# One of four input slots moved 128 B off a multiple of 512 B, in a batched matmul that is bound by its transfers

## The chip, the cores and the metric

The kernel runs on one core of one Trainium2 chip. The metric is the device time of one execution in microseconds (us), the median of several runs. All quoted comparisons are between runs marked fast, made on the same chip in the same call, except where it is said that a run stands alone (its state is then unknown).

## The reference

```python
# a: (16, 512, 512) float32 as (batch, k, m);  b: (16, 512, 512) float32 as (batch, k, n)
def reference(a, b):
    return np.matmul(a.transpose(0, 2, 1), b).astype(np.float32)
```

The inputs are 33.55 MB and the output is 16.78 MB: 50.33 MB have to cross between memory and the core's SBUF.

## The kernel before

The 16 products are made in 8 pairs. A load brings one operand (a or b) of one pair, 2 MiB, into one of four input slots: 16 KiB on each of 128 partitions. VectorE casts it to bfloat16, TensorE multiplies, ScalarE takes the sums out of PSUM into an output tile, and when the loads are over the stores follow. All DMAs are issued by the sync engine (SP) and share one queue.

```python
NX = 4
done = pool.tile([1, 96], f32, name="done")          # 384 B; 24 columns are used
x_ts = [pool.tile([P, R, M], f32, name=f"x{j}") for j in range(NX)]      # P 128, R 8, M 512
abf_ts = [...]; bbf_ts = [...]; o_ts = [...]         # (cut)
...
for n in range(2, 2 * pairs):                        # load n: a if n is even, b if it is odd
    if n >= NX:
        nc.sync.wait_ge(s_in, n - NX + 1)            # the slot has been cast
    nc.sync.dma_start(x_ts[n % NX][:], in_v[n % 2][n // 2]).then_inc(s_x[n % NX], 16)
...
nc.vector.wait_ge(s_x[n % NX], 16 * (n // NX + 1))   # for each pair (cut)
nc.vector.tensor_copy(out=(bbf_ts if n % 2 else abf_ts)[v][:],
                      in_=x_ts[n % NX][:, v * RV:(v + 1) * RV, :]).then_inc(s_cast, 1)
```

The slots begin at multiples of 512 B within a partition. Four small constants take 128 B ahead of the flag tile `done`, and its 384 B make up the rest.

Of the kernel before, what the change touches and what calls it, by code (L numbers as in the profile page):

```python
# [8 lines left out]
def kernel(  # L9
# [7 lines left out]
    P = 128  # L17
    batch, K, M = a.shape
    _, _, N = b.shape
    f32 = mybir.dt.float32  # L20
# [7 lines left out]
    R = K // Q  # L28
# [14 lines left out]
    NX = 4  # L43
# [4 lines left out]
    pool = ctx.enter_context(tc.tile_pool(name="sb", bufs=1))  # L48
# [2 lines left out]

    done = pool.tile([1, 96], f32, name="done")
    dve_done, act_done = done[:, 0:2 * pairs], done[:, 2 * pairs:3 * pairs]
    x_ts = [pool.tile([P, R, M], f32, name=f"x{j}") for j in range(NX)]
    abf_ts = [pool.tile([P, RV, M], bf, name=f"abf{v}") for v in range(V)]
    bbf_ts = [pool.tile([P, RV, N], bf, name=f"bbf{v}") for v in range(V)]
    o_ts = [pool.tile([P, G, T, N], f32, name=f"o{j}") for j in range(NO)]
# [157 lines left out]
```

## Time and profile before

| | before |
|---|---|
| median of the runs beside the first measurement | 123.78 us |
| span in the profile | 122.0 us |
| time of all DMA packets, share of 16 engines' span | 97.8% |
| packets of 16,384 B in the 14 full loads | 1,792 (8 a load and engine), median 611 ns |
| last product out of PSUM, last store landed | 94.0 us, 121.1 us |

The page tells which resource is full: a share near 100% for the DMA engines and about half for TensorE. The trace also keeps a record of each DMA packet (start, duration, size) and the time of each of the sixteen increments by which a DMA's semaphore tells that it has landed (the last of them is the landing). Among the packets are 448 of 4 B, sixteen for each of the 28 DMAs; I read them as the sending of these increments, one by each engine when it is through with its part.

### The profile page before, as it was taken

Reading aid. Unit: us, or ns where it says so; the run is one execution under the profiler, and the core shown is the slowest. Engines: PE = TensorE matmul, PEld = TensorE weight load, DVE = VectorE, ACT = ScalarE, POOL = GpSimd, SP = SyncE. Lnnn points to the kernel's source line nnn. Section 1 sums busy time; section 2 is a strip of 40 time slices with the busy share of each in tenths; the row PEclk is TensorE's granted clock in tenths of the full one; section 3 lists DMA queues with packets and bytes.
Section 4 is the critical chain, followed back from the end, with each engine's and each line's share of the span. In section 5 each row is a group of like instructions: output and inputs, shape, how many; then the busy total and the mean of one; then the engine's idle time right before and its main releaser. Section 6 shows DMA issues by size and latency. Waiting matters only on the chain. (4 is left out here: it accounts for less than half of the span.)

```text
span 122.0 us, 1208 instructions
## 1 busy us (share of the span) xinstructions
PE 63.6 (52%) x480; PEld 35.2 (29%) x480; DVE 37.9 (31%) x48; ACT 32.1 (26%) x41; POOL 0.2 (0%) x4
## 2 busy tenths in 40 slices
PE   0006928379969649979919928946991000000000
PEld 0002304135546325636606605612550000000000
DVE  0042070680494092474355437419000000000000
ACT  4000332400570830191570390191048000000000
POOL 0000000000000000000000000000000000000000
PEclk9999999958999995999999999995899855555555
DMA  4999999999999999999999999999999999999994
GB/s 97 363 424 430 448 430 440 430 430 435 435 430 435 430 430 430 430 430 430 430 430 430 435 430 430 430 365 430 430 422 430 427 430 427 427 430 427 430 430 180
DMA packets 5056, 50.33 MB, mean 412 GB/s; under 512 B 448, under 2 KB 448, under 8 KB 960
## 3 DMA queue, kind: packets, MB, share of 16 engines
q1 hardware_dynamic: 5056, 50.33, 97.8%
HBM read 33.55 MB, written 16.78 MB: 412 GB/s over the span
## 5 line engine op out<-in xcount | busy, mean ns | idle before, releaser
L147 PE MATMUL ps<-bbf,abf 64*128 64x512 bf16 x448 | 54.3, 401 | 15.3 <-PEq L142 15.3
L147 PEld LDWEIGHTS ps<-bbf,abf 64*128 64x128 bf16 x448 | 31.4, 114 | 38.2 <-issue 23.5
L172 ACT COPY o<-ps 128x1024 f32<-128x1024 f32 x28 | 26.3, 1027 | 43.9 <-PE ps L147 43.9
L109 DVE CAST abf<-x 128x2048 bf16<-128x2048 f32 x14 | 17.1, 1224 | 17.4 <-PE ps L147 13.4
L109 DVE CAST bbf<-x 128x2048 bf16<-128x2048 f32 x14 | 17.1, 1224 | 16.5 <-DMA x<-in_b_dram 16.5
L127 PE MATMUL ps<-bbf,abf 128*128 128x512 bf16 x32 | 9.3, 456 | 13.1 <-PEq L125 13.1
L127 PEld LDWEIGHTS ps<-bbf,abf 128*128 128x128 bf16 x32 | 3.8, 124 | 18.1 <-issue 16.2
L166 ACT COPY o<-ps 128x1024 f32<-128x1024 f32 x4 | 4.1, 1014 | 17.2 <-PE ps L127 17.2
L93 DVE CAST abf<-x 128x2048 bf16<-128x2048 f32 x2 | 2.5, 1228 | 11.9 <-PE ps L127 6.0
L93 DVE CAST bbf<-x 128x2048 bf16<-128x2048 f32 x2 | 2.4, 1224 | 1.7 <-DMA x<-in_b_dram 1.7
L177 ACT ACTIVATE done<-done 1x1 uint32<-1x1 uint32 x8 | 1.6, 197 | 0.0
L166 ACT ACT_TABLE_LOAD x1 | 1.3, 1283 | 0.9 <-SPq L71 0.9
L115 DVE MEMSET done<- 1x1 f32 x14 | 0.8, 59 | 0.0
L97 DVE MEMSET done<- 1x1 f32 x2 | 0.1, 59 | 0.0
L199 POOL MEMSET const-uint8-127<- 128x1 uint8 x1 | 0.1, 102 | 0.0
L199 POOL MEMSET const-bfloat16-1.0<- 128x1 bf16 x1 | 0.1, 101 | 0.0
L199 POOL MEMSET const-float32-0.0<- 128x1 f32 x1 | 0.1, 98 | 0.2 <-issue 0.2
L199 POOL MEMSET const-float32-1.0<- 128x1 f32 x1 | 0.1, 98 | 0.0
## 6 DMA issues: line engine op xcount, KB each, us to landing
out_dram<-o SPq DMA_DIRECT2D x8, 2048.0 KB, 25.0
x<-in_a_dram SPq DMA_DIRECT2D x7, 2048.0 KB, 12.1
x<-in_b_dram SPq DMA_DIRECT2D x7, 2048.0 KB, 15.9
x<-in_a_dram SPq DMA_DIRECT2D x1, 1024.0 KB, 8.4
x<-in_b_dram SPq DMA_DIRECT2D x1, 1024.0 KB, 10.4
x<-in_a_dram SPq DMA_DIRECT2D x1, 768.0 KB, 4.5
x<-in_b_dram SPq DMA_DIRECT2D x1, 768.0 KB, 6.5
x<-in_a_dram SPq DMA_DIRECT2D x1, 256.0 KB, 2.7
```

Of the source, the lines that this page charges most:

```text
L93: nc.vector.tensor_copy(out=bf_ts[0][:], in_=x_ts[j][:, u * RV:(u + 1) * RV, :]).then_inc(s_cast, 1)
L97: nc.vector.memset(dve_done[:, j:j + 1], 0.0).then_inc(s_in, 1)
L109: nc.vector.tensor_copy(out=(bbf_ts if n % 2 else abf_ts)[v][:], in_=x_ts[n % NX][:, v * RV:(v + 1) * RV, :],).then_inc(s_cast, 1)
L115: nc.vector.memset(dve_done[:, n:n + 1], 0.0).then_inc(s_in, 1)
L127: mm = nc.tensor.matmul(ps_ts[0][h][:, t % 2, :], a_m[:, r, t], bbf_ts[0][:, r, :], start=(r == 0), stop=(r == RV - 1),)
L147: mm = nc.tensor.matmul(ps_ts[g][h][:, t % 2, :], a_m[:, t], bbf_ts[v][rows, r, :], start=(v == 0 and r == 0), stop=(v == V - 1 and r == R ...
L166: nc.scalar.copy(out=o_ts[0][:, g, 2 * h:2 * h + 2, :], in_=ps_ts[0][h][:]).then_inc(s_ev[h], 1)
L172: ev = nc.scalar.copy(out=o_ts[i % NO][:, g, 2 * h:2 * h + 2, :], in_=ps_ts[g][h][:])
L177: nc.scalar.memzero(act_done[:, i:i + 1]).then_inc(s_out, 1)
L199: nc = _bacc.Bacc("TRN2", target_bir_lowering=False, num_devices=1)
```

## The change

The intent is to see what the start address of an input slot within a partition is worth, with everything else left in place. The second gap restores the alignment of what lies behind.

```diff
-    x_ts = [pool.tile([P, R, M], f32, name=f"x{j}") for j in range(NX)]
+
+    x_ts = [pool.tile([P, R, M], f32, name=f"x{j}") for j in range(NX - 1)]
+    pool.tile([1, 32], f32, name="gap0")
+    x_ts.append(pool.tile([P, R, M], f32, name=f"x{NX - 1}"))
+    pool.tile([1, 96], f32, name="gap1")
```

## The prediction

> **What bounds the kernel now.** I read the page first, then the view of waits of the queue that issues the DMAs, then the chain of work that ended last, then the windows view by stage, the source view of the load line, and at the end the trace's record of every DMA packet.
>
> ```profile
> PE 63.6 (52%) x480; PEld 35.2 (29%) x480; DVE 37.9 (31%) x48; ACT 32.1 (26%) x41; POOL 0.2 (0%) x4
> DMA  4999999999999999999999999999999999999994
> GB/s 97 363 424 430 448 430 440 430 430 435 435 430 435 430 430 430 430 430 430 430 430 430 435 430 430 430 365 430 430 422 430 427 430 427 427 430 427 430 430 180
> DMA packets 5056, 50.33 MB, mean 412 GB/s; under 512 B 448, under 2 KB 448, under 8 KB 960
> q1 hardware_dynamic: 5056, 50.33, 97.8%
> ```
>
> No compute engine is busy for much over half of the 122.0 us, while the DMA engines are busy in every slice but the first and the last, at 97.8% over the span. They move 430 GB/s nearly throughout. So this is a DMA-bound kernel from the third slice to the end, and any time added to the packets is added to the end, if nothing else leaves a gap in the queue.
>
> ```profile
> 94.02 0.06 ACT done L177
> ```
>
> The chain view's last entry is ScalarE's last flag, at 94.0 us, 28 us before the end. What follows is only the wait for the stores:
>
> ```profile
> SPq L80 <- DVE done L115: 44.0, 10, 8.3
> SPq L210 <- DMA out_dram<-o: 26.4, 1, 26.4
> ```
>
> Loads do wait for slots (44.0 us in ten waits), but the windows view shows that this waiting is ahead of need: the DMA share stays at 1 in each stretch.
>
> ```profile
> 40.00:50.00 10.00, 7.33 (x54) 4.01 (x51) 3.71 (x6) 3.82 (x5) 0.00 (x0) 0.83 1.03 442
> 78.00:82.00 4.00, 2.65 (x26) 1.39 (x21) 0.54 (x2) 3.07 (x4) 0.00 (x0) 1.00 0.94 375
> 94.00:110.00 16.00, 0.00 (x0) 0.00 (x0) 0.00 (x0) 0.07 (x2) 0.00 (x0) 0.58 1.01 428
> ```
>
> The last three columns are the clock of TensorE, the DMA share and GB/s. Only 78 to 82 us is under full rate: there the last load ends and the first store begins. The source view of the load line confirms the lead:
>
> ```profile
> DMA to landing us min/median/max: 10.9/14.6/19.0
> ```
>
> A 2 MiB load by itself takes 4.9 us, so each is issued two to four loads ahead of its landing.
>
> The packet records give the unit of cost. A full load is 128 packets of 16,384 B, 8 on each of 16 engines, and a packet takes 611 ns (median of 1,792). Packets of 8,192, 6,144 and 2,048 B take 309, 234 and 84 ns. That is a line: 8 to 9 ns fixed, and 1.177 ns for each 32 B ((611 - 309) / 256). At 16,384 B there are 512 such steps. There is no sign of a cost per 256 or 512 B beyond the steps themselves. All input slots now begin at multiples of 512 B, as the change says, so the trace has no misaligned load to look at.
>
> **What the Trainium skill says.** First, "DMA: Bandwidth & Descriptors", section "Where 436 GB/s comes from": 16 ports x 32 B x 850 MHz is 435.2 GB/s, so 1.176 ns for each 32 B. The trace agrees: 1.177 ns a step, and 430 GB/s in most slices. The kernel before sits on that ceiling. Second, the same page, section "How a descriptor splits into AXI transactions": a descriptor is cut into transactions of 256 B that begin at multiples of 256 B. One that begins off such a multiple has a first piece from the boundary below and a leftover at the end, and the bytes ahead of the start still cost beats. Its examples are about fetching; the write side isn't told apart, and no run so far shows either. Third, "SBUF — State Buffer", section "Operand start alignment": DMAs put the intended bytes at any element-aligned address, and "these runs timed nothing". It is about legality, so it says only that the result stays right. Fourth, "DMA: Bandwidth & Descriptors", section "Specifications": transfers under 512 B are done as read-modify-write. No data packet here is under 2 KB, so the trace shows nothing of that.
>
> **The change part by part.** It adds no instruction, removes none and moves no wait. It adds 128 B before the fourth input slot and 384 B behind it, 512 B together, so all tiles behind keep their place relative to 512 B. The memory is there, since no tile shrinks.
>
> What changes is the destination of one slot. Slots are used in turn, four of them, and there are 16 operand loads (two of them split in three parts). The fourth slot therefore takes loads 3, 7, 11 and 15: four loads of b, not the last alone. That is 4 x 2 MiB = 8.4 MB of the 50.3 MB, or 4 x 8 = 32 packets of 16,384 B on each engine: 32 x 611 ns = 19.6 us of DMA time. The HBM side of these loads keeps its alignment, and so do all stores.
>
> By the second place of the skill a 16,384 B packet that begins 128 B past a multiple of 256 B touches 65 pieces of 256 B and not 64. At worst each packet pays one piece more: 611 / 64 = 9.5 ns. 32 packets x 9.5 ns = 0.31 us. If only the half piece of bytes at an edge is paid, it is 0.15 us, and if the writes carry no unused bytes (128 B is four whole steps of 32 B), it is zero.
>
> Beside the DMA: VectorE reads this slot in 8 casts (v = 0 and 1 of four pairs) of 1,224 ns. The operand stays aligned to its elements and contiguous, so I give this zero; if a cast did grow, VectorE is 31% busy and issues loads about two loads ahead of need. Nothing of the DMA cost is hidden, though. The queue is one and first-in first-out in practice, always filled, so slower packets push every later load and every store. The last store is issued at 94.2 us and its data does not begin to move until about 116.6 us (the six stores before it must go first), so the compute tail has some 22 us to spare and hides nothing and adds nothing. The sum is 123.78 + 0.31 = 124.09, and I say 124.1 us.
>
> **The rivals.**
>
> First: every piece pays, not the packet's edge alone. The data arrive from HBM in aligned pieces of 256 B and each must be written across a boundary, as 128 + 128 B. If each cut costs one dead step, a packet gains 64 x 1.177 = 75 ns, 32 packets 2.4 us, and the time is 126.2 us. With three dead steps for each it is 7.2 us and 131.0 us. If the write rate halves, it is 19.6 us and 143.3 us. Against this: the packets of four sizes show a pure cost by 32 B steps, so pieces of 256 B go without a gap now, and 128 B is a whole number of steps. For it: nothing in the trace shows a misaligned write, the DMA has no slack to hide one, and somebody rounded the little flag tile up to 96 columns where it uses 24, which is what brings the slots to multiples of 512 B. That looks like a choice made for a reason.
>
> Second: the partial 512 B at each end of a row is done as read-modify-write. Two small ends a packet, if not overlapped, might cost as much as two of the smallest data packets seen, 2 x 84 ns (an estimate). Then 32 x 168 ns = 5.4 us and 129.2 us. Against: packets follow each other and such an end should overlap with the next packet.
>
> Third: nothing at all is seen, or a little gain. Only the ends could gain: the fixed 9 ns of 32 packets is 0.29 us, and the dip to 365 GB/s in one slice of 3.05 us at the last load is worth 65 / 430 x 3.05 = 0.46 us, if the new offset happened to remove it. So even the best case is about 123.0 us, 0.6%, and faster by over 2% is as good as excluded.
>
> Fourth: only the last load matters, because it alone gates the last products. Then a slower load would be hidden in the 22 us to spare. I don't believe it: its DMA time is in the queue before the stores.
>
> **Range and chances.** The main step gives 123.8 to 124.1, and run-to-run spread is 0.1 us. The first and second rival pull up, to 126 to 131 and in a tail further. I take 64% for a cost of under 2.4 us (edges, nothing, or a fraction of a dead step for each piece), 35% for over 2%, and 1% for a gain over 2%. The range is 123.5 to 130.0; what lies above it is the case of a write rate that falls by a third or more for this slot.
>
> **What would show it.** Right: the 16,384 B packets of loads 3, 7, 11 and 15 at 611 to 621 ns, the spacing of landings of these loads 4.9 us, slices all near 430 GB/s, the same packet count, casts at 1,224 ns. Wrong, first rival: these four loads alone lengthen by the same amount each, with four stretches of lower GB/s at a DMA share that stays at 1, and the span grows by their sum. Second rival: the same four, by a fixed amount a packet, which a half-size packet would show too. Wrong in another way: other loads or the stores change, or the queue runs dry (a DMA share under 1 in mid-span), which would mean that the lead of two loads is not enough; or more packets of another size, if the descriptors are cut differently at the new address.

## The result, and the profile after

The changed kernel took 123.63 us (median of four runs, 123.48 to 123.75) against 123.78 us (123.69 to 123.82). The ratio is 0.9988 with a 95% interval of 0.9971 to 1.0005: the same. A ratio is the mean time of one kernel's fast runs over that of the other's in the same rounds, so it isn't quite the ratio of the medians.

The page of the changed kernel, the lines on busy time, DMA by slice, packets and the queue:

```profile
PE 64.9 (53%) x480; PEld 35.3 (29%) x480; DVE 38.0 (31%) x48; ACT 32.1 (26%) x41; POOL 0.2 (0%) x4
DMA  4999999999999999999999999999999999999994
GB/s 96 364 435 427 462 430 430 430 430 435 430 430 430 430 430 430 430 430 430 430 430 430 430 430 435 424 373 427 430 422 430 430 430 427 427 430 427 427 430 180
DMA packets 5057, 50.33 MB, mean 413 GB/s; under 512 B 449, under 2 KB 449, under 8 KB 961
q1 hardware_dynamic: 5056, 50.33, 97.8%
```

The data packets are as many as before and the DMA share is the same; the one packet more belongs to another queue (instructions). One caution on the GB/s row: 430 in a slice of 3.05 us is 80 packets of 16,384 B, so the row moves by whole packets, in steps of about 5 GB/s, and can't show a difference of half a per cent.

The waits of the issuing queue:

```profile
SPq L84 <- DVE done L119: 43.1, 10, 8.8
SPq L214 <- DMA out_dram<-o: 27.1, 1, 27.1
```

The last entry of the chain that ended last:

```profile
92.59 0.06 ACT done L181
```

These answer to 44.0 us, 26.4 us and 94.0 us before. The loads still wait for slots far ahead of need. The compute tail ended 1.4 us earlier, which bought nothing, because the stores behind it were still in the queue: the last one landed at 121.0 us, against 121.1 us before.

The windows view of the changed kernel; the last columns are the TensorE clock, the DMA share and GB/s:

```profile
78.00:82.00 4.00, 4.00 (x40) 2.58 (x36) 1.37 (x2) 1.43 (x2) 0.00 (x0) 1.00 0.96 379
94.00:110.00 16.00, 0.00 (x0) 0.00 (x0) 0.00 (x0) 0.00 (x0) 0.00 (x0) 0.52 1.01 429
```

The dip where the last load meets the first store is there as before (379 GB/s against 375), so the offset did not remove it. The packet records say the rest. In loads 3, 7 and 11, which go to the moved slot, every one of the 384 packets takes 611 ns, as do all packets of the other full loads but the last. The sharpest look is at the time between two landings in the moved slot, which a cast of b waits for. The timeline of VectorE, casts of loads 7 and 11, first before, then after:

```profile
42.90 1.23 DVE L109 CAST bbf<-x 128x2048 bf16<-128x2048 f32 x1 [3.33 <-DMA x<-in_b_dram]
...
62.35 1.23 DVE L109 CAST bbf<-x 128x2048 bf16<-128x2048 f32 x1 [3.34 <-DMA x<-in_b_dram]
```

```profile
42.84 1.23 DVE L113 CAST bbf<-x 128x2048 bf16<-128x2048 f32 x1 [2.81 <-DMA x<-in_b_dram]
...
62.29 1.23 DVE L113 CAST bbf<-x 128x2048 bf16<-128x2048 f32 x1 [1.77 <-DMA x<-in_b_dram]
```

The first column is the start in us. 62.35 - 42.90 and 62.29 - 42.84 are both 19.45 us for a round of four loads. The edges that the prediction charged would have shown as 8 x 9.5 ns = 0.08 us in this difference, and the step here is 0.01 us.

### The profile page after: what moved, and what is told of

Its sections match the earlier page's. It is cut to its first block, busy times and chain, and to the rows that moved or that the text cites. A ratio compares the mean times of both kernels' runs of the same rounds, so it can differ in the third digit from the quotient of the medians.

```text
span 122.0 us, 1208 instructions
## 1 busy us (share of the span) xinstructions
PE 64.9 (53%) x480; PEld 35.3 (29%) x480; DVE 38.0 (31%) x48; ACT 32.1 (26%) x41; POOL 0.2 (0%) x4
## 5 line engine op out<-in xcount | busy, mean ns | idle before, releaser
L151 PE MATMUL ps<-bbf,abf 64*128 64x512 bf16 x448 | 53.0, 394 | 12.6 <-PEq L146 12.6
L113 DVE CAST abf<-x 128x2048 bf16<-128x2048 f32 x14 | 17.1, 1224 | 19.5 <-PE ps L151 13.9
L113 DVE CAST bbf<-x 128x2048 bf16<-128x2048 f32 x14 | 17.1, 1224 | 13.4 <-DMA x<-in_b_dram 13.4
L131 PE MATMUL ps<-bbf,abf 128*128 128x512 bf16 x32 | 11.9, 553 | 13.0 <-PEq L129 13.0
L97 DVE CAST bbf<-x 128x2048 bf16<-128x2048 f32 x2 | 2.4, 1224 | 1.8 <-DMA x<-in_b_dram 1.8
```

Source lines behind the costliest of these rows:

```text
L97: nc.vector.tensor_copy(out=bf_ts[0][:], in_=x_ts[j][:, u * RV:(u + 1) * RV, :]).then_inc(s_cast, 1)
L131: mm = nc.tensor.matmul(ps_ts[0][h][:, t % 2, :], a_m[:, r, t], bbf_ts[0][:, r, :], start=(r == 0), stop=(r == RV - 1),)
L151: mm = nc.tensor.matmul(ps_ts[g][h][:, t % 2, :], a_m[:, t], bbf_ts[v][rows, r, :], start=(v == 0 and r == 0), stop=(v == V - 1 and r == R ...
```

## The experiments

The question was whether an offset costs nothing at all or costs something that this kernel hides. Theory 1 is that only whole steps of 32 B count. The rivals are an edge paid by each packet, a cost by every piece, and a gain. Out of the first batch came theory C: the writing side does pay, but makes up for it in the loads to the slots that are not off.

**Once more, with five rounds.** No edit: the changed kernel.

> The changed kernel once more, beside the kernel before on the same chip, to see whether the 0.15 us by which it was quicker is real. If a 128 B offset costs and gains nothing (theory 1): ratio 1.000 within 0.001, every 16,384 B packet of loads 3, 7, 11 and 15 at 611 ns. If there is a small gain by the offset (theory 2): again about 0.9988, with an interval below 1. If an edge is paid (theory 3, as predicted): up to 1.0025.

Measured: 123.91 us against 123.88 us; the ratio is 0.997 (0.9929 to 1.0011). The runs of the kernel before spread over 123.59 to 125.32 us, so the interval is wide. The packets of loads 3, 7 and 11 took 611 ns, all of them. The 0.15 us of the first measurement is not shown to be a gain: the medians are level here, and both intervals hold 1.

**All four slots 128 B off.** Each slot gets 128 floats more, and a view of it begins 32 floats in:

```diff
-    x_ts = [pool.tile([P, R, M], f32, name=f"x{j}") for j in range(NX)]
+    OFF = 32
+    raw_ts = [pool.tile([P, R * M + 128], f32, name=f"x{j}") for j in range(NX)]
+    x_ts = [t[:, OFF:OFF + R * M].rearrange("p (r m) -> p r m", r=R) for t in raw_ts]
```

> All four input slots begin 128 B past a multiple of 512 B: four times the dose. Theory 1 (the write side counts whole steps of 32 B and an offset of four steps costs nothing): 16,384 B packets at 611 ns in all 14 full loads, the 2,048, 6,144 and 8,192 B packets at 84, 234 and 309 ns, time within 0.1% of before. Theory 3 (an edge of 9.5 ns a packet, hidden by chance in one slot): 14 x 8 packets x 9.5 ns = 1.1 us more for the full loads, 124.9 us. Theory 2 (a gain by the offset): about 4 x 0.15 = 0.6 us less.

Measured: 124.20 us against 123.88 us; ratio 0.9992 (0.995 to 1.0033). But the packets moved: their mean rises from 612.8 and 612.1 ns in the first two full loads to 614.6 ns in loads 6 to 14. So theory 1 falls, and the edge of theory 3 exists at 3.6 ns, not at 9.5 ns (the spacing of the slots changed as well; it is tested below).

**All four slots 4 B off.** The same edit with `OFF = 1`.

> All four input slots begin 4 B past a multiple of 512 B, so no write of a load begins at a whole step of 32 B. Theory 1a (a packet is streamed and only its edges are partial): one step more a packet, 1.2 ns, 14 x 8 x 1.2 = 0.13 us, which is in the noise; packets at 611 to 613 ns. Theory 1b (each 256 B piece from the source is written apart, and touches 9 steps of 32 B for 8): 64 x 1.177 = 75 ns a packet, 8.4 us in all, about 132 us, packets at 686 ns. Casts may be slower at 4 B past, which the slack of the load queue would hide.

Measured: 124.45 us against 123.88 us; ratio 1.0015 (0.9973 to 1.0056). Packets take 616.6 ns in the mean, 5.6 ns more, in nearly all loads from the first. Theory 1b (75 ns) falls, and theory 1a, which gave 611 to 613 ns, is too small. So 4 B, which breaks the 32 B step, costs 2.0 ns more than 128 B, and the casts still take 1,224 to 1,225 ns.

**Reading 128 B further in memory**, slots at multiples of 512 B, wrong result:

```diff
-            nc.sync.dma_start(x_ts[n % NX][:], in_v[n % 2][n // 2]).then_inc(s_x[n % NX], 16)
+            src = in_v[n % 2][n // 2]
+            if n < 2 * pairs - 2:
+                flat = (a, b)[n % 2].rearrange("b k m -> (b k m)")
+                at = (n // 2) * G * K * M + 32
+                src = flat[at:at + G * K * M].rearrange("(p r m) -> p r m", p=P, r=R)
+            nc.sync.dma_start(x_ts[n % NX][:], src).then_inc(s_x[n % NX], 16)
```

> Wrong result on purpose: 12 of the 14 full loads read 128 B further in memory, the slots stay at multiples of 512 B. The fetch side, of which the skill's examples speak. If the bytes ahead of the start cost beats: 512 + 4 steps, 616 ns a packet, 12 x 8 x 4.7 = 0.45 us more. If a whole piece is paid: 620 ns and 0.9 us. If only whole steps count: 611 ns and no change.

Measured: 123.85 us against 123.88 us; ratio 0.9968 (0.9915 to 1.0021). The median packet takes 611 ns in each load. Some packets are longer (up to 751 ns), but loads 4, 5, 8 and 9, all read off, are at 611 ns to the last packet. No cost of the bytes ahead of the start is to be seen on the fetching side. Whether it is absent or hidden behind another limit, no run here tells.

**A control for the spacing.** The wide spacing with `OFF = 0`.

> A control for the two kernels with all four slots off: the same spacing of the slots as there (16,896 B and not 16,384 B), but all slots at multiples of 512 B. If the 3.5 ns more a packet of the kernel with all slots at 128 B comes from the offset (theory A): 611 ns for all full loads here, and the time as before. If it comes from the spacing of the slots (theory B): about 614.5 ns here too.

Measured: 123.64 us against 123.89 us; ratio 0.9981 (0.9929 to 1.0033). All full loads but the last are at 611 ns. The spacing costs nothing.

**All four slots off in the tight spacing:**

```diff
-    done = pool.tile([1, 96], f32, name="done")
+    done = pool.tile([1, 128], f32, name="done")
...
     x_ts = [pool.tile([P, R, M], f32, name=f"x{j}") for j in range(NX)]
+    pool.tile([1, 96], f32, name="gap1")
```

> All four slots 128 B past a multiple of 512 B, in the spacing of the kernel before (16,384 B). Theory A (the offset): mean 614 to 615 ns a packet in the full loads after the first few, 0.3 to 0.4 us more in all. Theory B (the spacing): 611 ns and no change.

Measured: 123.99 us against 123.89 us; ratio 0.9999 (0.9946 to 1.0052). Packets take 614.6 ns in loads 6 to 14, as with the wide spacing, after two loads still at 611 ns. So it is the offset (theory A), and it takes some loads until it shows. The timelines of VectorE, loads 7 and 11 once more, first of the control, then of the tight kernel with all slots at 128 B, then of the one with all at 4 B:

```profile
42.51 1.23 DVE L111 CAST bbf<-x 128x2048 bf16<-128x2048 f32 x1 [3.33 <-DMA x<-in_b_dram]
...
61.96 1.23 DVE L111 CAST bbf<-x 128x2048 bf16<-128x2048 f32 x1 [3.34 <-DMA x<-in_b_dram]
```

```profile
43.09 1.23 DVE L110 CAST bbf<-x 128x2048 bf16<-128x2048 f32 x1 [3.37 <-DMA x<-in_b_dram]
...
62.68 1.23 DVE L110 CAST bbf<-x 128x2048 bf16<-128x2048 f32 x1 [3.37 <-DMA x<-in_b_dram]
```

```profile
43.34 1.23 DVE L111 CAST bbf<-x 128x2048 bf16<-128x2048 f32 x1 [3.39 <-DMA x<-in_b_dram]
...
62.99 1.23 DVE L111 CAST bbf<-x 128x2048 bf16<-128x2048 f32 x1 [3.39 <-DMA x<-in_b_dram]
```

A round of four loads takes 19.45, 19.59 and 19.65 us. The 0.14 and 0.20 us over 32 packets are 4.4 and 6.2 ns a packet, with a rounding of 0.3 ns. These are times of the engine that is last. In the mean of the sixteen engines, from the 4 B packets of load 7 to those of load 11, a round takes 19,449 ns before, and 19,577 and 19,651 ns here: 4.0 and 6.3 ns a packet. That is a little more than the packets' own durations show (3.6 and 5.6 ns). The records of neighbouring packets overlap by some 3 ns, so the count from start to start is the surer one.

**Two slots of four 128 B off** (the third and the fourth; `gap0` one slot earlier, and the gap behind as in the change).

> The third and the fourth slot 128 B off, so two loads off are followed by two that are not. If the cost of a load that is off is paid at once, packets of these loads take about 614.5 ns and the others 611 ns. If the write side lags behind and makes up for it in the loads that are not off (theory C, the reason for which one slot of four showed nothing), all packets take 611 ns still, or only the second load off grows a little. If it can't make up, the cost per load off appears from mid-run on, and in aligned loads too.

Measured: 123.79 us in one run, where the kernel before had a median of 123.89 us. All packets from load 4 to load 14 take 611 ns. But the lag grows from round to round. The lag of a load is the time from an engine's 4 B packet to its increment, in the mean of the sixteen engines. For loads 3, 7 and 11 it is 388, 410 and 428 ns. Over the nine pairs of loads to the same slot between load 2 and load 14, it grows by 17 to 22 ns a round, 19 ns in the mean. In the kernel before the same three lags are level at 341 to 343 ns, in the changed one at 359 to 362 ns. So the cost of loads that are off is there, but nothing waits for it yet.

(The expectation of the three-slot run below says 30 ns. That came from the end of the last of a load's 128 packets in order of start. The sixteen engines stand 0.4 to 1.2 us apart in these runs, in all but one kernel more than the 0.6 us of a packet, so packets of the next load get into that count. The lags in this text are by the 4 B packets, whose loads are 4.9 us apart and can't be mixed up.)

**One slot 4 B off** (wide spacing, the fourth slot alone with an offset of one float).

> Only the fourth slot is off, by 4 B and not by 128 B, spacing 16,896 B. With all four slots off by 4 B a packet took 616.6 ns in the mean, 5.5 ns more. Theory C (made up for in the three loads that follow): 611 ns in all loads. If a load off by 4 B is paid at once: 616.6 ns in loads 3, 7, 11 and 15 and 611 ns in the others, 32 x 5.5 = 0.18 us in all.

Measured: 123.88 us in one run. Loads 3, 7 and 11 are at 611 ns to the last packet and their lag is level. The lag shows both halves of theory C. In the load that is off it is 29 ns above that of the kernel before in the same slot, and in the three loads that follow 18, 13 and 1 ns above: it is paid back before the next load that is off. The changed kernel, 128 B off, shows the same with 18, 8, 1 and 1 ns. So one load off in four costs nothing in time, by 4 B as by 128 B.

**Three slots of four 128 B off** (`gap0` behind the first slot).

> Three of the four slots 128 B off. A forecast from theory C with the numbers so far. With all four off, a packet takes 614.6 ns, 3.6 ns more than the 611 ns at which packets are read. With two of four off the lag from the last packet to the landing grew by some 30 ns for each round of four loads, 16 x (3.6 - r), which gives r = 1.7 ns a packet that a slot not off makes up. Three of four: the lag grows by 8 x (3 x 3.6 - 1.7) = 73 ns a round at first, and once there is no room for more, packets take 611 + (3 x 3.6 - 1.7) / 4 = 613.3 ns in the mean. If the cost is paid by each load for itself: 614.6 ns in loads of slots 1, 2 and 3 and 611 ns in those of slot 0. If nothing short of all four costs: 611 ns.

Measured: 124.64 us in one run, against a median of 124.36 us. The forecast held in its sum, not in its order of lag first and packets later. From loads 2 to 5 to loads 6 to 9 the lag grew by 32 ns (73 forecast), and the packets of loads 6 to 9 took 613.2, 612.4, 611.2 and 611.4 ns already: together 32 + 8 x (2.2 + 1.4 + 0.2 + 0.4) = 66 ns (a few of these packets were held up, to 682 ns at most, as single packets of aligned kernels are too). From loads 6 to 9 to loads 10 to 13 the lag grew by 27 ns, while the packets of loads 10 to 13 grew to 613.1, 613.6, 611.4 and 611.5 ns, 612.4 ns in the mean (613.3 forecast). Both together are 27 + 8 x (2.1 + 2.6 + 0.4 + 0.5) = 72 ns a round. So the forecast sum holds, and the room for the lag was filling up. Neither "each load pays for itself" nor "only all four cost" fits. Load 12 goes to the slot that is not off, and load 13 directly behind it is off and still short of paying. The timelines of loads 7 and 11, with two slots off and with three:

```profile
42.95 1.23 DVE L112 CAST bbf<-x 128x2048 bf16<-128x2048 f32 x1 [3.37 <-DMA x<-in_b_dram]
...
62.42 1.23 DVE L112 CAST bbf<-x 128x2048 bf16<-128x2048 f32 x1 [3.35 <-DMA x<-in_b_dram]
```

```profile
43.09 1.23 DVE L112 CAST bbf<-x 128x2048 bf16<-128x2048 f32 x1 [2.70 <-DMA x<-in_b_dram]
...
62.63 1.23 DVE L112 CAST bbf<-x 128x2048 bf16<-128x2048 f32 x1 [1.67 <-DMA x<-in_b_dram]
```

A round takes 19.47 and 19.54 us. With 19.45 us for none and for one, and 19.59 us for four, this is how the time of a round answers to the number of slots that are off.

| kernel | slots off, by | mean packet, loads 10 to 13 | lag of loads 3, 7, 11, mean of the engines |
|---|---|---|---|
| before | none | 611.0 ns | 342, 341, 343 ns |
| control, wide | none | 611.0 ns | 342, 340, 343 ns |
| changed | one, 128 B | 611.0 ns | 362, 359, 360 ns |
| one slot, wide | one, 4 B | 611.0 ns | 370, 371, 371 ns |
| third and fourth | two, 128 B | 611.0 ns | 388, 410, 428 ns |
| second to fourth | three, 128 B | 612.4 ns | 408, 441, 467 ns |
| all, tight | four, 128 B | 614.6 ns | 470, 477, 478 ns |
| all, wide | four, 128 B | 614.6 ns | 452, 482, 482 ns |
| all, wide | four, 4 B | 616.6 ns | 463, 464, 463 ns |

The lag of an aligned load depends on its slot and hardly on the kernel: in the four kernels with all input slots aligned it is 339 to 348 ns for loads 3 and 4 and those to the same slots, and 319 to 325 ns for the other two slots (load 15 left out). So the level can be read too. With one or two slots off the lag stays at or under 428 ns, and packets keep 611 ns from load 4 on, but for two stray ones. With three slots off it goes from 416 to 469 ns in loads 6 to 14, and packets grow in part of the loads. With all four 128 B off it comes to rest at 475 to 483 ns from load 5 on, while every load pays.

**Short rows, slots at multiples of 512 B**, as a magnifier for a cost by edges. The loads of the fourth slot come in runs of 512 B; the cast and its wait follow suit (cut):

```diff
+            if n % NX == NX - 1:
+                dst = x_ts[n % NX][:].rearrange("p r m -> p (r m)").rearrange("p (h r m) -> p h r m", h=4, r=R)
+                src = in_v[n % 2][n // 2].rearrange("p r (h m) -> p h r m", h=4)
+                for h in range(4):
+                    nc.sync.dma_start(dst[:, h], src[:, h]).then_inc(s_x[n % NX], 16)
+                continue
```

> A magnifier, slots at multiples of 512 B: the four loads of the fourth slot are brought in runs of 512 B (32 for each partition) by four issues each, and the cast puts them in order again, so the result stays right. By the line of packet times, 8.5 ns + 16 x 1.177 ns = 27.3 ns a packet, 256 a load and engine: 7.0 us a load for 4.9, and 4 x 2.1 = 8.4 us more in all, 132 us. It is the base for the next one.

Measured: 127.95 and 128.54 us in two fast runs, 134.39 and 134.74 us in two slow. In the profiled fast run a load in short rows takes 6.05 us from the landing before it to its own, where 7.0 us was expected, so the base came out lower than the sum of its packet times.

**Short rows, the fourth slot 128 B off**: the same edit on the changed kernel.

> The same runs of 512 B, with the fourth slot 128 B off as in the changed kernel. If an offset of 128 B costs 3.6 ns for each packet on the write side (an edge): 256 x 4 x 3.6 = 3.7 us more than with the slot at a multiple of 512 B, less what the other loads make up. If a whole further piece of 256 B is paid for each packet: 9.5 ns and 9.7 us more. If the cost is by bytes and not by edges (3.6 ns for 16,384 B): nothing to be seen. If partial 512 B are read and written back, far more, 20 us and up.

Measured: 132.42 to 132.80 us in four fast runs; ratio to the kernel before 1.0657 (1.0613 to 1.07). Against the mean of the two fast runs at multiples of 512 B, 128.25 us, the mean of 132.66 us is 4.4 us more. That is 4.4 us / 1,024 packets = 4.3 ns a packet. This fits a cost by edges (3.7 us expected), and neither a cost by bytes (nothing) nor a read-modify-write (20 us and up). It isn't settled: the aligned kernel's own slow runs, at a granted clock of 0.83 and 0.84 like the fast ones (0.83 and 0.85), lie above these times, I don't know what makes them slow, and the profile of this kernel fell in a slow run, so I read no line of it.

**Output tiles 128 B off**, input slots aligned (a gap of 32 floats ahead of the output tiles).

> The output tiles 128 B off, the input slots at multiples of 512 B: stores read the slot off a multiple of 256 B. If fetching pays the bytes ahead of the start, as the skill's examples have it: 8,192 B packets of the stores at 309 + 4 x 1.177 = 314 ns, 128 x 4.7 = 0.6 us more in all. If the fetch side pays nothing, as loads from 128 B further in memory did not: 309 ns. ScalarE's evictions stay at 1,027 ns.

Measured: 123.89 us in one run, against a median of 124.36 us. The 8,192 B packets of the stores stay at 309 ns and the evictions at 1,026 ns. Reading a slot off a multiple of 256 B costs nothing that shows.

## Why the prediction was right or wrong

**The bound: right.** The kernel stayed bound by its transfers, the queue never ran dry and the compute tail had time to spare, which is seen in its ending 1.4 us earlier for nothing.

**The range and the chances: right.** 123.63 us lies in the range, and "within 2%" had the largest chance. It lies near the low end, though, under the 123.8 to 124.1 of the main step, whose cost was not there. The runs after it gave no reason for the 35% on slower: with rows of 16 KiB even four slots off stay within 0.6% by their intervals.

**The sum: one term too large.** The step "At worst each packet pays one piece more: 611 / 64 = 9.5 ns" gave 0.31 us. For one slot the term measured zero in the packets and in the time. An edge does exist, at 3.6 ns a packet when all four slots are off (4.0 ns from start to start). The lower ends that the same step named, 0.15 us and zero, were nearer. Two readings of the prediction are slightly off, and nothing hangs on them: (611 - 309) / 256 is 1.180 ns and not 1.177, and when the last store is issued five of the seven stores ahead of it have still to land, not six, and its own first packets start at 115.4 us and not 116.6.

**The step that failed** is "Nothing of the DMA cost is hidden". It holds for the queue, which has no gap, but not within a transfer. A packet whose write costs some ns more does not hold up the next packet at once: what shows is a later landing. In the changed kernel the lag is 18 ns higher after the load that is off, 8 ns after the next one and 1 ns after that, and the round takes the same 19.45 us. That is why one slot shows nothing in the packets or in the time. The two-slot run gives the net of a round. Its lag grows by 19 ns for 16 packets off and 16 not, so 16 x (3.6 - r) = 19 and the rate r at which aligned loads make up is about 2.4 ns a packet (an estimate from these two numbers). Three slots off should then cost 8 x (3 x 3.6 - 2.4) = 67 ns a round, and 66 and 72 ns were measured. Within a round the rates are rough: one load off should add 8 x 3.6 = 29 ns, and 18 were seen. That the lag is a lag of writes behind reads is my reading of it. The records show when a packet ends and when its DMA lands, not which side of the transfer they time. What sets the room for this lag, some 140 to 160 ns above the lag of aligned loads in the same slot, stays open as well. With all slots 4 B off it is a little smaller (460 to 465 ns) though a packet costs more.

**The first rival** (each piece of 256 B pays, 75 ns a packet) is refuted even at 4 B off, where a packet takes 5.6 ns more. **The second** (read-modify-write of both ends, 168 ns a packet) is refuted by the same numbers. **The third** (nothing, or a little gain) is what happened, as nothing. Neither ratio of the changed kernel shows a gain, and the dip at the last load stayed. **The fourth** (a slower last load is hidden behind the compute tail) was not put to work: loads 3, 7 and 11 were not slower to begin with, long before the tail.

The suspicion that the flag tile was rounded to 96 columns for a reason found no support of size. With all four slots off the ratio is 0.9999. The 3.6 ns x 8 packets x 14 loads would be 0.40 us, but part is given back: the packets of the last load, which meets the first store, take 642 ns in the mean in the kernel before and 615 ns in that one, 8 x 27 ns = 0.2 us (615 to 617 ns in the three kernels with all four slots off, 628 to 670 ns in the others with rows of 16 KiB; why is not shown).

## What to carry to other kernels

Where rows are long, the start of a tile within a partition is not worth a search: all input slots off cost 0.6 to 0.9% of a packet at 16 KiB a row (3.6 to 5.6 of 611 ns), and one in four cost no time. It may be edges that count and not bytes: with rows of 512 B the same offset in one slot seems to cost some 3% of the whole kernel (4.4 us of 128.25 us, not settled). And a resource that is busy all the time can still hide a small cost, as the lag of the landings did here, so try the full dose before an effect is called absent. When packets of several engines are counted by load, look for a mark that closes each engine's part: order of start mixes loads.

## What the Trainium skill lacked or had wrong

- "DMA: Bandwidth & Descriptors", section "How a descriptor splits into AXI transactions", doesn't say whether its account holds for writes into SBUF. For rows of 16,384 B written 128 B off a multiple of 256 B the runs show 3.6 ns more a packet (4 B off: 5.6 ns) when all loads are off, and no change of the packets when one of four is.
- The same section has the bytes ahead of an unaligned start cost beats in fetching. Here loads that read 128 B further in memory kept a median of 611 ns, where four beats more would be 616 ns, and stores that read SBUF 128 B off kept 309 ns. So the cost didn't show in either; whether another limit hid it isn't shown.
- "SBUF — State Buffer", section "Operand start alignment", says that its runs timed nothing. For VectorE's cast from float32 to bfloat16 of 128x2048 a source 4 B or 128 B off a multiple of 512 B took 1,224 to 1,225 ns, as an aligned one did.
- No page gives a figure for how far the landing of a load can fall behind its packets while these keep their rate. With two of four slots off the mean lag was 388, 410 and 428 ns over three rounds at 611 ns a packet, against 342 ns with none, and with all four off it came to rest at 475 to 483 ns.
